# mLSTM's running maxima spread over the partitions by way of memory, attention masks joined to the maximum on VectorE

## The chip, the core and the metric

The kernel runs on one core of one Trainium2 chip. TensorE (PE) multiplies, VectorE (DVE), ScalarE (ACT) and GpSimd (POOL) compute elementwise and reduce, SyncE (SP) issues most of the loads. Each engine works through its own queue in order, and an instruction at the head of a queue that waits for another engine holds up everything behind it on that engine. The metric is the device time of one execution in microseconds (us).

## What is computed

One decoder layer on 256 positions of width 1024: three mixers side by side (a pooling mixer, an mLSTM with 4 heads, a block attention with 8 heads), an output product, and a feed-forward part with a short convolution. What the change touches are the mLSTM's decay weights and the attention's softmax. Cut to that:

```python
def step(carry, inp):                       # mLSTM, per head
    g = jnp.cumsum(lf, axis=-1)
    logd = jnp.where(causal, g[..., :, None] - g[..., None, :] + ic[..., None, :], -jnp.inf)
    inter = g + m[..., None]
    mt = jnp.maximum(inter, jnp.max(logd, axis=-1))
    w = jnp.einsum('bhtd,bhsd->bhts', qc, kc) * jnp.exp(logd - mt[..., None])
    ...
# attention, per head; at 256 positions there is one block, so the causal own block is all of it
    s_own = jnp.einsum('bhqd,bhkd->bhqk', qi, k_own) * scale
    s_own = jnp.where((kpos[None, :] <= qpos[:, None])[None, None], s_own, -jnp.inf)
    p = jax.nn.softmax(jnp.concatenate([s_sel, s_own], axis=-1), axis=-1)
```

With a(s) = i(s) - g(s) and M(t) the running maximum of a, a decay weight is exp(a(s) - M(t)) for s up to t, and 0 behind it.

## The kernel before

**Products.** Every float32 weight is split on ACT and DVE into a high part (`hi`, line 184) and a rest (`lo`, line 191), and each product is three matmuls: high by high, high by rest, rest by high. Weights come in units of about 1 MB by SP's queue into four buffers; a unit's load is issued when the rest of the unit four before it is made. The input product has eleven units ("of", "vi", "pool", "mq", "mk", "akA", "aqA", "akB", "aqB", "avA", "avB"); each is 4 blocks of 12 matmuls, called bulk blocks here. After them stand the output product (`wo`), the up product (`upr`, `up`) and the down product (`dn`).

**Order.** Between the bulk blocks the mixers' smaller work is woven in by hand. `put(key, f, *after)` registers a piece, the table `PLACE` gives it a number, and the pieces are emitted sorted by that number (a bulk block n has the number n). So one number sets where a piece's instructions come in the queue of every engine that it uses. The framework adds the semaphores and hands out buffers.

**mLSTM.** `gate_scans` (key "gs") makes, on 4 partitions, one per head, the running maximum `mr`. The decay weights need -M(t) on all 128 partitions (one partition per s, t along the row). For that `gate_hi` and `gate_lo` split `mr`, and for each head `decay_t` (keys ("pm", h)) runs four matmuls: a selector `sel_m` of -1 by the two parts, 384 columns each, and twice an identity by a bfloat16 mask of 128 columns. `decay` (("wt", h)) takes the exponential on ACT from PSUM into `wt`. `mscore_t` (("mS", j)) multiplies queries and keys of two heads, `mscore` (("me", h)) joins scores and decay on DVE, `mnum_t` (("mN", t)) multiplies by the values. `sigmoids` and `silu` make queries and keys ready; the sigmoids need a table load on ACT before and after.

**Pooling.** `pool_z` runs two chains of small adds on POOL, first j = 0, then j = 1; `pool_t` (("ply", j)) multiplies each result `pld` on PE, first j = 1, then j = 0.

**Attention.** `score_t` (("S", g, j)) makes scores of two heads: four float32 matmuls of 64 rows (two of 128 columns, two of 256) and four mask matmuls (identity by a bfloat16 mask, 128 columns). `prob_max` (("mx", g, j)) takes the row maxima on DVE straight from PSUM, `prob_exp` (("ex", g, j)) the exponentials on ACT from PSUM into `pr`, then come the division, the transposes (`PT`) and the product with the values (`O`). The masks and the selector come by one load into `con0` and are cast on POOL in `setup`.

Of the kernel before, what the change touches and what calls it, by code (L numbers as in the profile page):

```python
# [9 lines left out]
F32 = mybir.dt.float32  # L10
# [26 lines left out]
    "n1g": 3.714, "n1n": 4.567, "rbt": 6.601, "rb": 9.429, ("of", 0): 6.981, ("of", 1): 6.014, ("vi", 0): 6.19,  # L37
    ("vi", 1): 7.571, "setup": 3.741, "gain": 13.052, "pg": 7.69, "ga": 9.023, "gm": 9.583, "gs": 9.638, "gh": 9.938,
    "gl": 11.815, "gc": 11.24, "gco": 12.693, "gce": 15.533, ("ply", 0): 26.237, ("plh", 0): 26.457,
    ("pll", 0): 26.931, ("ply", 1): 22.154, ("plh", 1): 26.706, ("pll", 1): 27.325, ("plz", 0): 10.439,  # L40
# [10 lines left out]
    ("mlo", 1): 38.548, ("hq", "akA", 0): 21.853, ("hs", "akA", 0): 23.338, ("hq", "akA", 1): 23.685,  # L51
# [1202 lines left out]
```

## Time and profile before

| | |
|---|---|
| time, median of 3 runs | 314.48 us (314.48 to 314.83) |
| the profiled execution's own time | 314.26 us |
| its span, first to last instruction | 312.6 us |
| PE busy in the span | 308.1 us (99%) |
| DVE busy | 227.1 us (73%) |
| ACT busy | 186.0 us (59%) |
| POOL busy | 16.5 us (5%) |
| granted TensorE clock | 1.000 |

The profiled execution takes 1.66 us more than its span; that lies around it. Busy time is the time in which at least one instruction of the engine runs. Matmuls overlap: the 128x256 bulk matmul is listed with 0.28 us, but one starts every 0.12 us. So what a matmul costs on PE is read from the start of one row to the start of the next, not from its length. The mixers lie between 8 and 120 us, the up product up to 248 us, the down product behind it.

### The profile page before, as it was taken

Reading aid. Unit: us, or ns where it says so; the run is one execution under the profiler, and the core shown is the slowest. Engines: PE = TensorE matmul, PEld = TensorE weight load, DVE = VectorE, ACT = ScalarE, POOL = GpSimd, SP = SyncE. Lnnn points to the kernel's source line nnn. Section 1 sums busy time; section 2 is a strip of 40 time slices with the busy share of each in tenths; the row PEclk is TensorE's granted clock in tenths of the full one; section 3 lists DMA queues with packets and bytes.
Section 4 is the critical chain, followed back from the end, with each engine's and each line's share of the span. In section 5 each row is a group of like instructions: output and inputs, shape, how many; then the busy total and the mean of one; then the engine's idle time right before and its main releaser. Section 6 shows DMA issues by size and latency. Waiting matters only on the chain.

```text
span 312.6 us, 5639 instructions
## 1 busy us (share of the span) xinstructions
PE 308.1 (99%) x2251; PEld 283.7 (91%) x2251; DVE 227.1 (73%) x427; ACT 186.0 (59%) x366; POOL 16.5 (5%) x30
## 2 busy tenths in 40 slices
PE   8999999999999999999999999999999999999995
PEld 5999899989977789999999999999999988888885
DVE  1779898898746676689988888788788786534112
ACT  4986669688577536858566475565664594425000
POOL 0026910000000000000000000000000000000000
PEclk9999999999999999999999999999999999999999
DMA  7997553321703670161564464563555549800003
GB/s 227 424 411 282 191 214 136 134 66 72 268 2 136 240 297 2 39 232 53 217 229 177 148 236 156 173 235 134 204 200 151 228 151 368 316 0 2 0 0 134
DMA packets 8825, 53.81 MB, mean 172 GB/s; under 512 B 984, under 2 KB 1248, under 8 KB 2784
## 3 DMA queue, kind: packets, MB, share of 16 engines
q1 hardware_dynamic: 8512, 52.95, 45.6%
q10 hardware_dynamic: 288, 0.52, 0.6%
q8 instruction: 17, 0.28, 0.4%
q14 instruction: 8, 0.07, 0.1%
HBM read 52.42 MB, written 1.05 MB: 171 GB/s over the span
## 4 chain that ended last, share of the span: by engine, by line
PE 99%; DVE 0%; issue 0%
PE dn L842 20%; PE up L313 12%; PE up L311 12%; PE up L312 12%; PE wo L842 7%; PE warm L331 1%; PE upr L320 1%; PE upr L322 1%; PE upr L321 1%; PE of L455 1%; PE n1pt L350 1%; PE aqA L320 1%; PE mq L311 1%; PE mk L311 1%; PE akB L320 1%; PE vi L322 1%
## 5 line engine op out<-in xcount | busy, mean ns | idle before, releaser
L191 DVE TENSOR_TENSOR lo<-raw,hi 128x1024 fp32r<-128x1024 f32 (+2 forms) x102 | 116.1, 1158 | 24.7 <-ACT hi L184 24.6
L184 ACT ACTIVATE hi<-raw 128x1024 fp32r<-128x1024 f32 (+2 forms) x102 | 98.8, 994 | 28.5 <-PE dn L842 18.9
L311 PE MATMUL up<-h_hi,hi 128*128 128x256 f32 x320 | 90.4, 283 | 0.0
L313 PE MATMUL up<-h_hi,lo 128*128 128x256 f32 x320 | 90.3, 282 | 0.0
L312 PE MATMUL up<-h_lo,hi 128*128 128x256 f32 x320 | 90.1, 282 | 0.0
L311 PEld LDWEIGHTS up<-h_hi,hi 128*128 128x128 f32 x320 | 60.6, 189 | 0.0
L313 PEld LDWEIGHTS up<-h_hi,lo 128*128 128x128 f32 x320 | 60.5, 189 | 0.0
L312 PEld LDWEIGHTS up<-h_lo,hi 128*128 128x128 f32 x320 | 60.4, 189 | 0.0
L1103 DVE SCALAR_TENSOR_TENSOR fy<-up,par,fy 128x255 f32<-128x255 f32 x88 | 41.9, 481 | 14.9 <-ACT fy L1100 13.4
L1100 ACT ACTIVATE fy<-up,par 128x256 f32<-128x256 f32 x44 | 20.0, 465 | 31.9 <-PE up L313 31.9
L842 PE MATMUL dn<-hi,a_hi 128*128 128x512 f32 (+1 forms) x110 | 29.0, 349 | 0.0
L842 PE MATMUL dn<-hi,a_lo 128*128 128x512 f32 (+1 forms) x110 | 28.9, 348 | 0.0
L842 PE MATMUL dn<-lo,a_hi 128*128 128x512 f32 (+1 forms) x110 | 28.9, 348 | 0.0
L842 PEld LDWEIGHTS dn<-lo,a_hi 128*128 128x128 f32 x110 | 19.5, 188 | 2.9
L842 PEld LDWEIGHTS dn<-hi,a_lo 128*128 128x128 f32 x110 | 19.4, 188 | 2.9
L842 PEld LDWEIGHTS dn<-hi,a_hi 128*128 128x128 f32 x110 | 19.3, 188 | 2.9
L238 ACT ACTIVATE a_hi<-fy 128x256 fp32r<-128x256 f32 x22 | 9.2, 419 | 11.8 <-DVE fy L1109 11.8
L1152 DVE TENSOR_TENSOR xs<-dn,xs 128x512 f32<-128x512 f32 (+1 forms) x5 | 2.8, 583 | 16.5 <-PE dn L842 16.5
L842 PE MATMUL wo<-hi,mix_hi 128*128 128x512 f32 x32 | 11.4, 418 | 0.0
L842 PE MATMUL wo<-lo,mix_hi 128*128 128x512 f32 x32 | 10.7, 394 | 0.0
L842 PE MATMUL wo<-hi,mix_lo 128*128 128x512 f32 x32 | 10.6, 394 | 0.0
L239 DVE TENSOR_TENSOR a_lo<-fy,a_hi 128x256 fp32r<-128x256 f32 x22 | 9.2, 420 | 1.5 <-ACT a_hi L238 1.5
(307 smaller groups left out, 546.0 us busy)
## 6 DMA issues: line engine op xcount, KB each, us to landing
raw<-in_w SPq DMA_DIRECT2D x46, 1024.0 KB, 4.8
raw<-in_wg SPq DMA_DIRECT2D x2, 520.0 KB, 6.4
raw<-in_wg SPq DMA_DIRECT2D x1, 1040.0 KB, 8.8
out_y<-xs SPq DMA_DIRECT2D x3, 256.0 KB, 2.1
xs<-in_x ACTq DMA_DIRECT2D x2, 256.0 KB, 4.0
xs<-in_x SPq DMA_DIRECT2D x2, 256.0 KB, 4.0
con<-in_consts SPq DMA_DIRECT2D x1, 384.0 KB
par<-in_params SPq DMA_DIRECT2D x1, 337.0 KB, 10.6
```

The costliest lines, as they stand in the source:

```text
L184: nc.scalar.activation(hi_t[u][:, s], raw_t[u][:, s], AF.Copy)
L191: nc.vector.tensor_sub(lo_t[u][:, s], raw_t[u][:, s], hi_t[u][:, s].bitcast(F32))
L238: nc.scalar.activation(hi, src, AF.Copy)
L239: nc.vector.tensor_sub(lo, src, hi.bitcast(F32))
L311: nc.tensor.matmul(dst, a, h_hi[:, k, :], start=k == 0, stop=False)
L312: nc.tensor.matmul(dst, a, h_lo[:, k, :], start=False, stop=False)
L313: nc.tensor.matmul(dst, b, h_hi[:, k, :], start=False, stop=k == KT - 1)
L320: nc.tensor.matmul(dst, h_hi[:, k, ts_], hw[:, k, :], start=k == 0, stop=False)
L322: nc.tensor.matmul(dst, h_lo[:, k, ts_], hw[:, k, :], start=False, stop=k == KT - 1)
L842: nc.tensor.matmul(acc[t, c], a, b[:, k, o:o + n], start=st and i == 0, stop=sp and i == 2)
L1100: nc.scalar.activation(y, ps[j], AF.Copy, scale=pcol(c0 + 4 * NPAIR))
L1103: nc.vector.scalar_tensor_tensor(y[:, d:], ps[j][:, :S - d], pcol(c0 + 2 * NPAIR * tap), y[:, d:], op0=ALU.mult, op1=ALU.add)
```

## The change

The maxima no longer go through PE. `gate_scans` writes `mr` in another order, `spread_max` ("bm") stores it from POOL's queue to a buffer in memory, `spread_back` ("br") loads it from there, again from POOL's queue, as the same 1536 numbers into each of 128 partitions (786 KB, tile `mb`), and `mask_max` ("bs") sets the masked places with an AFFINE_SELECT on POOL, in place. `decay` takes the exponential in place of `mb`, with scale -1, and the scores are joined in `mb` too. `gate_hi`, `gate_lo` and `decay_t` go.

The attention's mask matmuls go as well. A mask of 256 columns is made once on POOL; `prob_max` becomes a TENSOR_TENSOR_REDUCE on DVE that adds the mask to the scores, writes the sum to `pr` in SBUF and takes the row maximum; `prob_exp` reads `pr` in place of PSUM. The load of `con0` goes, and the casts on POOL with it. Nearly all numbers of `PLACE` move a little.

```diff
-    ...("cy", "mk", 0): 19.109, ("ct", "mk", 0): 19.499, ("cz", "mk", 1): 19.365, ("cy", "mk", 1): 21.291,
...
+    "e": ..., ("hi", 1, 0): -2.6, "bm": 10.847, "br": 11.9, "bs": 13.467,
...
+    dpool = ctx.enter_context(tc.tile_pool(name="dpool", bufs=1, space=bass.MemoryType.DRAM))
...
-    nc.sync.dma_start(con0[:, :C_RCNT], consts[:, :C_RCNT])
-    nc.sync.dma_start(con, consts[:, C_RCNT:])
+    nc.sync.dma_start(con, consts)
...
+    mask = mpool.tile([P, S], F32, name="mask")
+    mb = mpool.tile([P, 3, 4, P], F32, name="mb")
...
-        nc.gpsimd.tensor_copy(mask_b, con0[:, C_MASK:C_MASK + 2 * P])
-        nc.gpsimd.tensor_copy(sel_m, con0[:4, C_SELM:C_SELM + 4 * P])
-        nc.gpsimd.tensor_copy(ident_b, ident)
+        nc.gpsimd.memset(mask, 0.0)
+        nc.gpsimd.affine_select(mask, mask, [[-1, S]], ALU.is_ge, NEG, base=P, channel_multiplier=1)
...
-    def gate_hi():
-        sb["mh"] = mpool.tile([4, 384], F32R, name="mh")
-        nc.scalar.activation(sb["mh"], sb["mr"], AF.Copy)
-
-    def gate_lo():
-        sb["ml"] = mpool.tile([4, 384], F32R, name="ml")
-        nc.vector.tensor_sub(sb["ml"], sb["mr"], sb["mh"].bitcast(F32))
+    def spread_max():
+
+        sb["far"] = dpool.tile([3, 4, P], F32, name="far")
+        nc.gpsimd.dma_start(sb["far"].rearrange("b h c -> h b c"), sb["mr"].rearrange("h (b c) -> h b c", c=P))
+
+    def spread_back():
+        nc.gpsimd.dma_start(mb, sb["far"].partition_broadcast(P))
+
+    def mask_max():
+
+        d = mb.rearrange("p b h c -> p (b h) c")[:, :8, :]
+        nc.gpsimd.affine_select(d, d, [[0, 8], [1, P]], ALU.is_ge, -NEG, base=0, channel_multiplier=-1)
...
-    def decay_t(h):
-
-        pm = aux([P, 384], f"pm{h}")
-        s = sel_m[:, h * P:(h + 1) * P]
-        nc.tensor.matmul(pm, s, sb["mh"], start=True, stop=False)
-        nc.tensor.matmul(pm, s, sb["ml"], start=False, stop=False)
-        for c in (0, S):
-            nc.tensor.matmul(pm[:, c:c + P], ident_b, mask_b[:, :P], start=False, stop=c == S)
-        ps_t["pm", h] = pm
-
     def decay(h):
-        pm = ps_t["pm", h]
-        e = mpool.tile([P, 384], F32, name=f"wt{h}")
-        nc.scalar.activation(e[:, :S], pm[:, :S], AF.Exp, bias=cols[:, 0, h:h + 1])
-        nc.scalar.activation(e[:, S:], pm[:, S:], AF.Exp, bias=cols[:, 1, h:h + 1])
+        e = mb[:, :, h, :]
+        nc.scalar.activation(e[:, 1:], e[:, 1:], AF.Exp, bias=cols[:, 0, h:h + 1], scale=-1.0)
+        nc.scalar.activation(e[:, 0], e[:, 0], AF.Exp, bias=cols[:, 1, h:h + 1], scale=-1.0)
         sb["wt", h] = e
...
     def score_t(g, j):
         q, k = sb["aq" + g, j], sb["ak" + g, j]
         pss = [aux([P, 384], f"S{g}{j}{half}") for half in range(2)]
-        for half in range(2):
-            hs = slice(64 * half, 64 * half + 64)
-            nc.tensor.matmul(pss[half][:, :P], q[hs, :P], k[hs, :P], start=True, stop=False)
-        for half in range(2):
-            nc.tensor.matmul(pss[half][:, :P], ident_b, mask_a, start=False, stop=True)
-        for half in range(2):
-            hs = slice(64 * half, 64 * half + 64)
-            nc.tensor.matmul(pss[half][:, P:], q[hs, P:], k[hs, :], start=True, stop=False)
-        for half in range(2):
-            nc.tensor.matmul(pss[half][:, S:], ident_b, mask_a, start=False, stop=True)
+        for o, t in ((slice(0, P), slice(0, P)), (slice(P, 384), slice(P, S))):
+            for half in range(2):
+                hs = slice(64 * half, 64 * half + 64)
+                nc.tensor.matmul(pss[half][:, o], q[hs, t], k[hs, :t.stop], start=True, stop=True)
...
     def prob_max(g, j):
...
+        pr = big(f"pr{g}{j}")[:, :768].rearrange("p (h c) -> p h c", c=384)
+        sb["pr", g, j] = pr
         for half in range(2):
             for t, s in spans:
-                nc.vector.tensor_reduce(mx[:, half, t:t + 1], pss[half][:, s], axis=AX.X, op=ALU.max)
+                nc.vector.tensor_tensor_reduce(pr[:, half, s], pss[half][:, s], mask[:, P - P * t:], 1.0, 3 * NEG,
+                                               op0=ALU.add, op1=ALU.max, accum_out=mx[:, half, t:t + 1])
...
     def prob_exp(g, j):
...
-                nc.scalar.activation(pr[:, half, s], pss[half][:, s], AF.Exp, bias=mx[:, half, t:t + 1],
+                nc.scalar.activation(pr[:, half, s], pr[:, half, s], AF.Exp, bias=mx[:, half, t:t + 1],
...
-    put("gh", gate_hi, "gs")
-    put("gl", gate_lo, "gh")
+    put("bm", spread_max, "gs")
+    put("br", spread_back, "bm")
+    put("bs", mask_max, "br")
...
-        put(("pm", h), do(decay_t, h), "gl", "setup")
-        put(("wt", h), do(decay, h), ("pm", h), "gco")
+        put(("wt", h), do(decay, h), "bs", "gco")
```

What the new numbers and pieces do to the engines' queues is seen at three places. In the rows below, an instruction stands with its line, its operation, what it writes and reads, and its shape; line numbers of the changed kernel are its own.

On PE, the first scores of the attention's second half (`SB`, two heads in two PSUM tiles), before:

```order
L322 MATMUL avA_1143<-hi_726,h_lo 128x256
L724 MATMUL SB_1197<-akBT_1166,aqBT_1163 128x128
L724 MATMUL SB_1198<-akBT_1166,aqBT_1163 128x128
L726 LDWEIGHTS ident_b
L726 MATMUL SB_1197<-mask_b,ident_b 128x128
L726 LDWEIGHTS ident_b
L726 MATMUL SB_1198<-mask_b,ident_b 128x128
L729 MATMUL SB_1197<-akBT_1166,aqBT_1163 128x256
L729 MATMUL SB_1198<-akBT_1166,aqBT_1163 128x256
```

and after:

```order
L318 MATMUL avB_1169<-hi_782,h_lo 128x256
L713 MATMUL SB_1184<-akBT_1136,aqBT_1085 128x128
L713 MATMUL SB_1185<-akBT_1136,aqBT_1085 128x128
L713 MATMUL SB_1184<-akBT_1136,aqBT_1085 128x256
L713 MATMUL SB_1185<-akBT_1136,aqBT_1085 128x256
L694 MATMUL hmT_1200<-ident,hm_835 128x128 x2
L316 MATMUL avB_1169<-hi_782,h_hi 128x256
```

The mask's four matmuls (two of them are behind the rows shown) are gone, the scores moved behind one more bulk block, and the mLSTM's transposes `hmT`, which stood by themselves before, now stand beside them. In the same way other woven-in pieces were put next to each other: outside the decay blocks, bulk work is broken into by 27 groups of small matmuls before and by 19 after.

On POOL, the end of pooling chain j = 0 (result `pld`) and the start of chain j = 1, before:

```order
L808 COPY plz_387<-plz_384 64x256
L811 TENSOR_TENSOR pld_391<-plz_387,con 128x256
L812 TENSOR_TENSOR pld_391<-pld_391,plz_381 128x256
L798 MEMSET plz_438 128x16
L804 MEMSET plz_441 128x16
L806 TENSOR_TENSOR plz_441<-plz_438 128x256
```

and after, where the second row of the round trip waits for the landing of the first:

```order
L792 COPY plz_372<-plz_369 64x256
L795 TENSOR_TENSOR pld_376<-plz_372,con 128x256
L796 TENSOR_TENSOR pld_376<-pld_376,plz_366 128x256
L605 DMA far<-mr 4x3x128
L608 DMA mb<-far 128x1536
L782 MEMSET plz_438 128x16
L788 MEMSET plz_441 128x16
L790 TENSOR_TENSOR plz_441<-plz_438 128x256
```

Both transfers now stand in the queue between the two chains; the AFFINE_SELECT on `mb` stands behind the second.

On ACT, the sigmoids (`sg`, between two table loads) and the decays, before:

```order
L642 ACTIVATE wt_645<-pm_562,cols 128x256
L643 ACTIVATE wt_645<-pm_562,cols 128x128
L524 ACTIVATE akAsq_651<-akA_616,n1r_236 128x256
L642 ACTIVATE wt_653<-pm_518,cols 128x256
L643 ACTIVATE wt_653<-pm_518,cols 128x128
L234 ACT_TABLE_LOAD
L494 ACTIVATE gm<-gm 128x256 x2
L497 ACTIVATE sg<-mqT_525 128x256
```

and after:

```order
L490 ACTIVATE sg<-mkT_617 128x256
L230 ACT_TABLE_LOAD
L630 ACTIVATE mb<-mb,cols 128x2x128
L631 ACTIVATE mb<-mb,cols 128x128
L630 ACTIVATE mb<-mb,cols 128x2x128
L631 ACTIVATE mb<-mb,cols 128x128
L517 ACTIVATE akAsq_653<-akA_587,n1r_253 128x256
```

All four heads' decays moved from ahead of the sigmoids to behind the second table load. On DVE each of the 16 maxima is two instructions now, the reduction and a read of its result (128x1).

## Rows read from the trace of the kernel before

**Rows 1.** The page, part 1: busy us (share) xinstructions of each engine.

```profile
PE 308.1 (99%) x2251; PEld 283.7 (91%) x2251; DVE 227.1 (73%) x427; ACT 186.0 (59%) x366; POOL 16.5 (5%) x30
```

**Rows 2.** Waits of PE: engine, line, waited for: us, times, longest.

```profile
PE warm L331 <- DVE idle L326: 1.3, 1, 1.3
```

**Rows 3.** Timeline of PE, first decay block: start us, length us, instruction, count.

```profile
30.39 0.28 PE L313 MATMUL mq<-h_hi,lo 128*128 128x256 f32 x1
30.60 0.44 PE L633 MATMUL pm<-mh,sel_m 4*128 4x384 f32 x1
...
31.24 0.36 PE L311 MATMUL mq<-h_hi,hi 128*128 128x256 f32 x1
31.44 0.28 PE L312 MATMUL mq<-h_lo,hi 128*128 128x256 f32 x1
31.55 0.28 PE L313 MATMUL mq<-h_hi,lo 128*128 128x256 f32 x1
```

**Rows 4.** Timeline of PE: one block of attention scores, and what follows.

```profile
82.28 0.49 PE L724 MATMUL SB<-akBT,aqBT 64*128 64x128 f32 x4
82.70 0.29 PE L726 MATMUL SB<-mask_b,ident_b 128*128 128x128 bf16 x2
82.92 0.70 PE L729 MATMUL SB<-akBT,aqBT 64*128 64x256 f32 x4
83.56 0.29 PE L731 MATMUL SB<-mask_b,ident_b 128*128 128x128 bf16 x2
83.65 0.36 PE L320 MATMUL avB<-hi,h_hi 128*128 128x256 f32 x1
```

**Rows 5.** Timeline of PE: the pooling product, and both blocks of mLSTM scores.

```profile
46.61 0.59 PE L817 MATMUL ply<-pld,par 128*128 128x256 f32 x2
...
49.98 0.93 PE L653 MATMUL mS<-mqT,mkT 64*128 64x256 f32 x8
50.84 0.39 PE L320 MATMUL aqA<-hi,h_hi 128*128 128x256 f32 x1
...
52.45 1.10 PE L653 MATMUL mS<-mqT,mkT 64*128 64x256 f32 x8
```

**Rows 6.** Timeline of POOL: ends of chain j = 0 and of chain j = 1.

```profile
30.57 1.62 POOL L812 TENSOR_TENSOR pld<-pld,plz 128x256 f32<-128x256 f32 x1
...
39.27 0.81 POOL L812 TENSOR_TENSOR pld<-pld,plz 128x256 f32<-128x256 f32 x1
```

**Rows 7.** DMA issues: tile, queue, count, KB each, median us to landing.

```profile
xs<-in_x ACTq DMA_DIRECT2D x2, 256.0 KB, 4.0
...
con<-in_consts SPq DMA_DIRECT2D x1, 256.0 KB, 12.7
out_y<-xs SPq DMA_DIRECT2D x2, 128.0 KB, 1.7
```

**Rows 8.** Timeline of DVE around the mLSTM's scores, with the idle time before a row.

```profile
28.44 0.96 DVE L614 TENSOR_TENSOR ml<-mr,mh 4x384 fp32r<-4x384 f32 x1
...
48.89 0.43 DVE L501 TENSOR_TENSOR mqT<-mqT,sg 128x256 f32<-128x256 f32 x1 [0.63 <-ACT sg L497]
...
51.70 0.42 DVE L530 TENSOR_REDUCE akAss<-akAsq 128x4 f32<-128x256 f32 x1
52.03 0.55 DVE L658 SCALAR_TENSOR_TENSOR wt<-mS,wt 128x384 f32<-128x384 f32 x1
52.49 0.17 DVE L535 TENSOR_SCALAR akAss<-akAss 128x8 f32<-128x8 f32 x1
```

**Rows 9.** Groups by line and shape: xcount, busy us, mean ns, idle us before.

```profile
L739 DVE TENSOR_REDUCE mxA<-SA 128x1 f32<-128x256 f32 x4 | 1.7, 414 | 0.0
...
L751 ACT ACTIVATION_READ_ACCUMULATOR prA<-SA,mxA,aqr 128x1 f32 x8 | 1.7, 210 | 0.0
...
L210 POOL TENSOR_SCALAR_AFFINE_SELECT ident<-ones 128x128 f32<-128x128 f32 x1 | 0.3, 292 | 0.1
```

**Rows 10.** One stretch: busy us of PE, PEld, DVE, ACT, POOL; clock; DMA share, GB/s.

```profile
28.00:75.00 47.00, 47.00 (x382) 43.50 (x381) 42.00 (x104) 35.93 (x80) 11.50 (x16) 1.00 0.43 157
```

More of the change, by code (lines that the diff above doesn't have):

```diff
@@ L36 @@
 PLACE = {
[L37 to L40, printed above, removed]
[10 rows of a table removed]
-    ("mlo", 1): 38.548, ("hq", "akA", 0): 21.853, ("hs", "akA", 0): 23.338, ("hq", "akA", 1): 23.685,
[44 rows of a table removed]
+    "n1g": 4.19, "n1n": 4.722, "rbt": 7.381, "rb": 8.32, ("of", 0): 6.657, ("of", 1): 5.837, ("vi", 0): 6.566,
+    ("vi", 1): 7.27, "setup": 3.875, "gain": 16.963, "pg": 7.867, "ga": 8.38, "gm": 9.124, "gs": 9.606, "gc": 10.156,
+    "gco": 12.183, "gce": 16.746, ("ply", 0): 26.237, ("plh", 0): 27.301, ("pll", 0): 27.489, ("ply", 1): 22.756,
+    ("plh", 1): 26.859, ("pll", 1): 27.39, ("plz", 0): 9.748, ("plz", 1): 12.359, ("cz", "mq", 0): 14.116,
[54 rows of a table added]
 }
@@ L108 @@
 N_UNITS = U_DOWN + N_DOWN
-C_MASK = 0
-C_SELM = C_MASK + 2 * P
-C_RCNT = C_SELM + 4 * P
+C_RCNT = 0
 C_END = C_RCNT + 2 * S
@@ L206 @@
     par = cpool.tile([P, Q_END], F32, name="par")
-    con0 = tpool.tile([P, D], F32, tag="big", name="con0", bufs=3)
-    con = mpool.tile([P, C_END - C_RCNT], F32, name="con")
+    con = mpool.tile([P, C_END], F32, name="con")
     nc.gpsimd.memset(ones, 1.0)
@@ L411 @@
     mix_lo = mpool.tile([P, KT, S], F32R, name="mix_lo")
-    mask_b = mpool.tile([P, 2 * P], BF16, name="mask_b")
-    mask_a = mask_b[:, P:]
-    sel_m = mpool.tile([4, 4 * P], F32R, name="sel_m")
-    ident_b = mpool.tile([P, P], BF16, name="ident_b")
+    mask = mpool.tile([P, S], F32, name="mask")
+    mb = mpool.tile([P, 3, 4, P], F32, name="mb")
     gg = mpool.tile([P, 1], F32, name="gg")
@@ L602, in gate_scans @@
         nc.vector.scalar_tensor_tensor(ar, ps_t["pg"][:, 0, :], b_i, gc, op0=ALU.add, op1=ALU.subtract)
-        nc.vector.tensor_tensor_scan(mr[:, :S], ar, ar, 0.0, op0=ALU.max, op1=ALU.max)
-        nc.vector.tensor_copy(mr[:, S:], mr[:, P:S])
-        nc.vector.tensor_add(gc, gc, mr[:, :S])
+        nc.vector.tensor_tensor_scan(mr[:, P:], ar, ar, 0.0, op0=ALU.max, op1=ALU.max)
+        nc.vector.tensor_copy(mr[:, :P], mr[:, S:])
+        nc.vector.tensor_add(gc, gc, mr[:, P:])
         sb["mr"] = mr
-    def gate_hi():
-        sb["mh"] = mpool.tile([4, 384], F32R, name="mh")
-        nc.scalar.activation(sb["mh"], sb["mr"], AF.Copy)
-    def gate_lo():
-        sb["ml"] = mpool.tile([4, 384], F32R, name="ml")
-        nc.vector.tensor_sub(sb["ml"], sb["mr"], sb["mh"].bitcast(F32))
+    def spread_max():
[6 more added lines that the diff above has]
+        nc.gpsimd.affine_select(d, d, [[0, 8], [1, P]], ALU.is_ge, -NEG, base=0, channel_multiplier=-1)
     def gate_cols_t():
@@ L647, in mscore_t @@
         for half in range(2):
-            ps_t["mS", 2 * j + half] = aux([P, 384], f"mS{2 * j + half}")
+            ps_t["mS", 2 * j + half] = aux([P, 3, P], f"mS{2 * j + half}")
         q, k = sb["mq", j], sb["mk", j]
-        for s, o in ((0, slice(0, S)), (1, slice(S, 384))):
+        for s, o in ((0, slice(1, 3)), (1, 0)):
             for half in range(2):
@@ L664, in mnum_t @@
             if t == 0:
-                nc.tensor.matmul(pn[:, h, :], e[:, :P], v_aug[:, 0, h, :], start=True, stop=True)
+                nc.tensor.matmul(pn[:, h, :], e[:, 1], v_aug[:, 0, h, :], start=True, stop=True)
             else:
-                nc.tensor.matmul(pn[:, h, :], e[:, P:S], v_aug[:, 0, h, :], start=True, stop=False)
-                nc.tensor.matmul(pn[:, h, :], e[:, S:], v_aug[:, 1, h, :], start=False, stop=True)
+                nc.tensor.matmul(pn[:, h, :], e[:, 2], v_aug[:, 0, h, :], start=True, stop=False)
+                nc.tensor.matmul(pn[:, h, :], e[:, 0], v_aug[:, 1, h, :], start=False, stop=True)
         ps_t["num", t] = pn
@@ L745, in prob_exp @@
     def prob_exp(g, j):
-        pss, rq, mx = ps_t["S", g, j], sb["rq", g], sb["mx", g, j]
+        pr, rq, mx = sb["pr", g, j], sb["rq", g], sb["mx", g, j]
         sm = tpool.tile([P, 2, NT], F32, tag="sm", name=f"sm{g}{j}")
-        pr = big(f"pr{g}{j}")[:, :768].rearrange("p (h c) -> p h c", c=384)
         for half in range(2):
             for t, s in spans:
-                nc.scalar.activation(pr[:, half, s], pss[half][:, s], AF.Exp, bias=mx[:, half, t:t + 1],
+                nc.scalar.activation(pr[:, half, s], pr[:, half, s], AF.Exp, bias=mx[:, half, t:t + 1],
                                      scale=rq[:, t, 2 * j + half:2 * j + half + 1],
@@ L1223, in _consts @@
     c = np.zeros((P, C_END), np.float32)
-    i = np.arange(P)
-    c[:, C_MASK:C_MASK + P] = np.where(i[None, :] >= i[:, None], 0.0, NEG)
-    c[:, C_MASK + P:C_MASK + 2 * P] = np.where(i[None, :] <= i[:, None], 0.0, NEG)
-    for h in range(4):
-        c[h, C_SELM + P * h:C_SELM + P * (h + 1)] = -1.0
     t = np.arange(S) + 1.0
```

108 rows, old and new, of the table PLACE are left out of this document.

## The prediction, made blind

> **What bounds the kernel now.** I read the busy times first: PE is busy 308.1 of 312.6 us [rows 1]. Then the waits: PE waited once, 1.3 us at the very start [rows 2]. Between 28 and 75 us, where all of the mLSTM and half of the attention lie, it is busy in all 47.00 us, and the granted clock is 1.00 [rows 10]. So PE sets the time, by its amount of work: what is taken from PE comes off the time, whatever moves to other engines is free as long as PE still finds its inputs, and each microsecond in which it doesn't is lost. The second thing to see is how near the next engine is: DVE is busy 42.0 of those 47 us [rows 10]. Third, the places where PE arrives just in time, since the change makes it arrive earlier.
>
> **What leaves PE.** *Decay blocks.* From the first selector matmul to the next bulk matmul 31.24 - 30.60 = 0.64 us pass [rows 3]. Bulk matmuls start every 0.11 us (31.44 to 31.55), but the block's first one starts 0.21 after the one ahead, and the second bulk matmul behind it 0.20 after the first: going from one kind of matmul to another costs 0.10 and 0.09 us more. A block is 0.83 us, and there are four: 3.3 us. If the switches stayed, 4 x 0.64 = 2.6.
>
> *Mask matmuls.* A score block takes 83.65 - 82.28 = 1.37 us [rows 4]. The mLSTM's scores are the same four matmuls (64 rows, twice 256 and twice 128 columns) without masks: 50.84 - 49.98 = 0.86 us [rows 5]. So 0.51 goes with the masks, 4 x 0.51 = 2.0 us. Least: the mask rows by themselves, (82.92 - 82.70) + (83.65 - 83.56) = 0.31 [rows 4], in all 1.2. Most: group A's two blocks stand side by side, so one pair of switches (0.19) can fall out besides, 2.2.
>
> *Pieces put side by side.* Bulk work is broken into 19 times, not 27. A break costs up to the 0.19 of two switches, 8 x 0.19 = 1.5; nothing where the neighbours differ in kind (transposes beside 64-row or 64-column matmuls), as in about half of these. I take 0.6, from 0 to 1.5.
>
> Together 3.3 + 2.0 + 0.6 = 5.9 us less work on PE (3.8 to 7.0).
>
> **What moves to GpSimd, and who waits.** The round trip stands in POOL's queue between the two pooling chains. The first transfer waits for `mr`, which is long there. The second waits for the landing of the first, and behind it in the queue stand chain j = 1 and then the AFFINE_SELECT. That chain's result is wanted first on PE, at 46.61 [rows 5]; now it is ready at 39.27 + 0.81 = 40.08 [rows 6], 6.5 us ahead. After the change PE comes there earlier by the decay blocks, all four of which lie ahead, and one merged break: 46.61 - 3.3 - 0.2 = 43.1. POOL comes later by the round trip: one issue, one landing, one more issue. No POOL transfer is in this trace. The nearest landing is a small write to memory by another queue, 1.7 us for 128 KB; a load of 256 KB took 4.0 [rows 7]. An issue costs POOL between nothing and its slowest add here, 1.62 [rows 6]. That is 1.7 to 7.2 us; as the transfer is 6 KB I stay near the short end, 3.5. Chain j = 0 ends at 30.57 + 1.62 = 32.2, chain j = 1 takes 40.08 - 32.2 = 7.9, so it ends at 32.2 + 3.5 + 7.9 = 43.6, and PE waits 0.5 (0 to 4.2).
>
> The page "DMA: Bandwidth & Descriptors" of the Trainium skill, section "Anatomy of one DMA — SWDGE (gpsimd) path", gives a transfer issued by GpSimd a fixed cost of about 2.0 us and attributes most of it to the write's receipt; no run here shows it yet. By it the chain would end near 43 and this wait would be nil.
>
> The AFFINE_SELECT takes 0.29 us for 128 columns [rows 9], so at most 8 x 0.29 = 2.3 for 1024, and the decays can start on ACT at about 46. They stand behind the sigmoids' second table load, so ACT is hardly sooner there. The load into `mb` has those 7.9 us of chain j = 1 to land; a quarter less than a weight unit, it is covered.
>
> **What moves on DVE.** `ml` goes, 0.96 us [rows 8]. Each of 16 maxima gets a read of its result. The nearest row for that is ACT's, 0.21; the reduction itself reads PSUM as before (0.41 for 256 columns) and now writes a row and reads a mask as well [rows 9]. I take 0.2 each, 3.2 us, half of it (1.6) in the crowded stretch; from 1.6 to 4.8 in all. Covered, in the second half, by the slack of a DVE that isn't full there; in the first by little.
>
> The place where it shows first is the second block of mLSTM scores. One of its PSUM tiles comes free when the first `mscore` is done; before, that ended at 52.49 [rows 8] with PE there at 52.45 [rows 5]: already just in time, its block 1.10 long where the first was 0.93. PE now comes 3.5 earlier, 48.95. On DVE, up to that point, `ml` goes (0.96), one head reduction moves behind it (51.70 to 52.03, 0.33), and part of the 0.63 that DVE waited for sigmoids [rows 8] and of its other idle time, 5.0 us in the stretch [rows 10]; the count of splits ahead of it (ten from 25 us on) is the same. So `mscore` ends 1.3 to 3.5 us earlier, say 2.3: at 50.2, and PE waits 1.2. This wait comes after the one for POOL and holds what is left of it, so the larger counts, not the sum: 1.2 us, from 0 to 4.2. ACT's exponentials read SBUF in place of PSUM, same size, no change taken. The load taken out (384 KB) and the one put in (786 KB) run beside loads that use 0.43 of the engines' time [rows 10]: 0.
>
> **The sum.** 5.9 - 1.2 = 4.7 us. On the profiled execution, 314.26 - 4.7 = 309.6 (span 312.6 - 4.7 = 307.9); the median of the runs lies 0.2 above it, so 314.48 - 4.7 = **309.8 us**. About 0.2% (0.6 us) is what a measurement of this kernel can tell from no change.
>
> **Rivals.** *All waits stay covered* (POOL's issues near nothing, DVE gains all of its idle time): 314.48 - 5.9 = 308.6, with the bounds of the work 307.5 to 308.6. For it: 6.5 us of margin now. Against: the 52.45 block is late already. Chance 0.15 for under 308.6.
>
> *The round trip becomes PE's wait.* A round trip of 6 us ends the chain at 46.1 and costs PE 3.0: 311.6; one of 7.2, the upper bound, 4.2: 312.8. For it: a landing and two issues that no row prices. Against: 6 KB, written while DMA is half free. Chance 0.15 for 311.4 to 313.8.
>
> *Slower: the landing is as long as at the start of the program*, where a 256 KB load took 12.7 us [rows 7]. POOL blocks for 12.7 + 1.6, chain j = 1 ends at 54.4, PE waits 11.3: 314.48 - 5.9 + 11.3 = 319.9. It decides from a round trip of 43.1 - 32.2 - 7.9 + 5.9 = 8.9 us on. Against: that load queued behind megabytes of others, while around 32 us the engines are half free [rows 10]. Chance 0.05.
>
> *No change: DVE becomes the bound.* It would, if the 5.0 us that it idles between 28 and 75 us are all chains that don't shrink. Then the stretch takes 47.0 - 1.0 + 1.6 = 47.6 and PE's savings in it are lost; behind it remain two score blocks and some merged breaks, about 1.3: 314.48 + 0.6 - 1.3 = 313.8, and with the maxima at their upper price (2.4) 314.6. For it: 42 of 47. Against: at least 0.63 of the idle time is a wait that the new order removes, and splits can slip to a later place, since they stand some microseconds ahead of their use. Chance 0.05.
>
> **How the numbers follow.** The forecast's own range, with waits up to 3 and the work's bounds, is 308.6 to 311.4, chance 0.60. With the covered case (0.15), the late round trip (0.15), the DVE case (0.05) and the slower one (0.05) all is counted. 8 in 10 need 308.0 to 312.6: that leaves out the far ends of the first two rivals, and both last. Faster by over 0.2% (under 313.85): 0.60 + 0.15 + 0.15 and a part of the DVE case, 0.91. Within 0.2%: 0.04. Slower: 0.05.
>
> **What would show it.** Between `mq` and `akA` PE has no breaks, so that `akA` starts near 38.9, not 42.3. A score block with no masks lasts 0.9, not 1.37. On POOL the gap between the end of chain j = 0 and the first add of chain j = 1 is the round trip: 3.5 expected. PE's waits then list `ply` on POOL with under 1 us and the second `mS` on DVE with 1 to 2; nothing else above 0.5. DVE's maxima with their reads cost 0.2 each more than before. The prediction is wrong if that gap is over 6, if PE waits at the attention's transposes or scores, or if the score blocks keep their 1.37 (then the masks' switches were not theirs).

## The result, and the profile after

| | before | after |
|---|---|---|
| median of the runs, us | 314.48 | 313.09 |
| profiled execution, span | 312.6 | 311.4 |
| PE busy in the span | 308.1 | 304.1 |

The ratio is 0.9946, 95% interval 0.9931 to 0.9962: 1.4 us faster (lowest run 312.29, highest 313.34). 309.8 was forecast, with a range up to 312.6; the direction was right, the size was not, and the time lies half a microsecond outside. One execution of `e9_mask_early` below, at a granted clock of 0.56 throughout and 494 us, is in no median.

First the busy times (columns as in [rows 1]) and the waits (as in [rows 2]) of the changed kernel:

```profile
PE 304.1 (98%) x2219; PEld 282.6 (91%) x2219; DVE 228.0 (73%) x442; ACT 186.4 (60%) x365; POOL 17.6 (6%) x32
```

```profile
POOL mb L608 <- DMA far<-mr: 5.3, 1, 5.3
...
PE ply L801 <- POOL pld L796: 2.7, 1, 2.7
```

PE has one new wait, the pooling product on POOL; beside the wait at the very start [rows 2], DVE appears nowhere in its list. POOL itself waits 5.3 us for the landing of `far`. Its timeline shows the round trip, between the end of chain j = 0, the two transfers, and chain j = 1 (compare [rows 6]):

```profile
32.48 1.61 POOL L796 TENSOR_TENSOR pld<-pld,plz 128x256 f32<-128x256 f32 x1
34.03 0.78 POOL L605 DMA_DIRECT2D far<-mr  x1
40.11 0.58 POOL L608 DMA_DIRECT2D mb<-far  x1 [5.30 <-DMA far<-mr]
...
40.89 0.61 POOL L790 TENSOR_TENSOR plz<-plz 128x256 f32<-128x256 f32 x1
...
45.35 0.78 POOL L796 TENSOR_TENSOR pld<-pld,plz 128x256 f32<-128x256 f32 x1
46.25 1.92 POOL L613 TENSOR_SCALAR_AFFINE_SELECT mb<-mb 128x1024 f32<-128x1024 f32 x1
```

From 34.09 to 40.68 is 6.6 us of round trip; chain j = 1 ends at 46.13. On PE's timeline the rows that answer to [rows 4] and [rows 5] are:

```profile
39.09 0.28 PE L316 MATMUL akA<-hi,h_hi 128*128 128x256 f32 x1
...
43.25 0.28 PE L318 MATMUL akA<-hi,h_lo 128*128 128x256 f32 x1
46.19 0.70 PE L801 MATMUL ply<-pld,par 128*128 128x256 f32 x2 [2.65 <-POOL pld L796]
...
48.10 0.41 PE L318 MATMUL akA<-hi,h_lo 128*128 128x256 f32 x1
48.31 0.41 PE L316 MATMUL akA<-hi,h_hi 128*128 128x256 f32 x1
...
83.50 0.93 PE L713 MATMUL SB<-akBT,aqBT 64*128 64x128 f32 x8
84.36 0.44 PE L694 MATMUL hmT<-ident,hm 128*128 128x128 f32 x2
```

`akA` begins at 39.09, where 38.9 was forecast; a score block lasts 84.36 - 83.50 = 0.86 us. So PE's work went as forecast. Then comes the wait, and a second loss: at 48 us bulk matmuls start every 0.21 us, not every 0.12. Two stretches of after (columns as in [rows 10]), and then one of the kernel before:

```profile
34.00:40.00 6.00, 6.00 (x53) 6.00 (x52) 5.75 (x11) 2.94 (x5) 0.81 (x2) 1.00 0.95 327
47.20:50.40 3.20, 3.20 (x17) 3.20 (x16) 3.20 (x5) 2.37 (x8) 0.97 (x1) 0.50 0.03 5
```

```profile
34.00:40.00 6.00, 6.00 (x47) 5.22 (x46) 5.02 (x8) 4.92 (x10) 5.69 (x8) 1.00 0.92 314
```

Behind the wait the granted clock is 0.50 (1.2 GHz) for about 3.4 us: 3.4 x (1 - 0.12 / 0.21) = 1.5 us lost. And the DMA engines are busy 0.95 of the stretch in which `far` is to land; they were busy 0.92 of it before the change too. At the place where the prediction put the transfer, 32.2 us, they were all but idle in the kernel before:

```profile
32.20:34.00 1.80, 1.80 (x14) 1.41 (x14) 1.80 (x3) 0.01 (x1) 1.73 (x5) 1.00 0.02 5
```

Between 31 and 34 us one weight load was issued before, at 33.4; in the changed kernel two are, at 31.8 and 33.5, and `far` comes at 34.03, behind both.

How much work left PE follows from a stretch that holds all of the change, from the first `mq` matmul to the transposes behind the mixer; first and last row of it, before and after:

```profile
27.54 0.39 PE L311 MATMUL mq<-h_hi,hi 128*128 128x256 f32 x1
...
132.75 0.49 PE L1056 MATMUL up<-ident,upc 128*128 128x128 f32 x3
```

```profile
27.68 0.28 PE L307 MATMUL mq<-h_hi,hi 128*128 128x256 f32 x1
...
131.35 1.18 PE L1040 MATMUL up<-ident,upc 128*128 128x128 f32 x8
```

It is 105.21 us long before and 103.67 after: 1.54 less, with 2.65 of wait and some 1.5 of half clock in it. That makes 5.7 us less work; 5.9 was forecast. The half clock in this sum is an estimate; the same stretch in three runs below in which the clock held gives 5.2 (`e1_swap_ply`), 5.3 (`e7_probes`) and 5.9 (`e2_fill`, without its fill).

### The profile page after: what moved, and what is told of

Same layout as the page of the kernel before. It is cut to its first block, busy times and chain, and to the rows that moved or that the text cites. A ratio compares the mean times of both kernels' runs of the same rounds, so it can differ in the third digit from the quotient of the medians.

```text
span 311.4 us, 5585 instructions
## 1 busy us (share of the span) xinstructions
PE 304.1 (98%) x2219; PEld 282.6 (91%) x2219; DVE 228.0 (73%) x442; ACT 186.4 (60%) x365; POOL 17.6 (6%) x32
## 4 chain that ended last, share of the span: by engine, by line
PE 90%; POOL 4%; DMA 2%; DVE 1%; ACT 1%; issue 1%; POOLq 0%
PE dn L826 20%; PE up L309 12%; PE up L307 12%; PE up L308 12%; PE wo L826 7%; POOL plz L790 2%; DMA far<-mr 2%; PE warm L327 1%; PE upr L316 1%; PE upr L318 1%; PE upr L317 1%; PE of L448 1%; PE n1pt L346 1%; PE aqA L316 1%; POOL pld L795 1%; POOL pld L796 1%
```

## Experiments

The theory from this profile: the work is gone, and 4.2 us of the gain are lost at one place, the wait for POOL and the fall of the clock behind it. The rivals: DVE would have taken the place of that wait; the clock fell for another reason; the landing is that long by itself. Medians are of five to twelve runs unless said; those of the kernel before beside them are 314.55 to 314.61.

### The attention's part alone, and the decays' part alone

`e4_attn_only` is the kernel before with these lines, and `prob_exp` reading `pr`:

```diff
-            nc.tensor.matmul(pss[half][:, :P], ident_b, mask_a, start=False, stop=True)
-            nc.tensor.matmul(pss[half][:, S:], ident_b, mask_a, start=False, stop=True)
-                nc.vector.tensor_reduce(mx[:, half, t:t + 1], pss[half][:, s], axis=AX.X, op=ALU.max)
+                nc.vector.tensor_tensor_reduce(pr[:, half, s], pss[half][:, s], mask[:, P - P * t:], 1.0, 3 * NEG,
+                                               op0=ALU.add, op1=ALU.max, accum_out=mx[:, half, t:t + 1])
```

> The kernel before, with only the attention masks changed as in the change: no mask matmuls in the score blocks, the mask added in the maximum's instruction on DVE, the exponential read from that row. Decays and order as before. Theory: each of four score blocks falls from 1.37 to 0.86 us, DVE's 16 maxima cost at most 0.2 each more and stay covered: 314.5 - 2.0 = 312.5 us. Rival: DVE, full in this stretch, holds PE by what it takes on (up to 3.2 us): 313.5 to 315, with a PE wait on DVE at the attention's transposes or scores.

312.84 us, ratio 0.9946 (0.9934 to 0.9958): 1.7 less. PE waits for nothing but at the start.

`e6_masks_too` is the changed kernel with the mask matmuls back on PE:

```diff
+            nc.tensor.matmul(pss[half][:, :P], ident_b, mask_a, start=False, stop=True)
+            nc.tensor.matmul(pss[half][:, S:], ident_b, mask_a, start=False, stop=True)
```

> The changed kernel, with the attention's mask matmuls put back on PE as in the kernel before, besides the masks on DVE, which stay (a place masked twice is as far below the maximum). This is the change without what it takes from PE in the attention. Theory: the two parts add up; four score blocks cost 0.51 more each, as the kernel before with only the attention changed gained 1.7: 313.1 + 1.7 to 2.0 = 314.8 to 315.1 us, so the decay part alone, with the waits it brings, gains nothing. Rival: PE's added work sits beside waits and part of it is covered: 313.5 to 314.5.

315.10 us, ratio 1.0026 (1.0003 to 1.0049), with a wait of 3.9 us for POOL. The two parts add up within the noise: the attention's part is worth 1.7; the rest, for all that it takes from PE (3.5 us in the profiled execution, by the stretch above), gains nothing and costs 0.5 (0.1 to 1.5). Its runs fall in two groups by the mean granted clock: six of 0.998 and over took 313.9 to 314.6, six of 0.995 and under 315.6 to 317.2. So whether the clock falls differs from run to run of one kernel, and even where it held the rest of the change gained at most 0.7.

### The clock and the wait

`e2_fill` gives PE something to do ahead of the late product:

```diff
         py = aux([P, S], f"ply{j}")
+        for _ in range(20 if j else 0):
+            nc.tensor.matmul(py, idle[:, :P], idle[:, :S], start=True, stop=True)
```

> The changed kernel, with twenty matmuls of 256 columns on zeros (about 2.1 us of PE) issued ahead of the pooling product of chain j = 1, into the tile that the product then overwrites. The wait for POOL is as long, but PE works through most of it. Theory: the fall of the granted clock to 0.5 from 47.1 to 50.5 us comes from PE's idle 2.7 us. Then the listed wait falls to about 0.5, the clock stays 1.00, the loss of 1.6 us goes and the wait itself stays: 311.5 us. Rival: the clock falls for another reason at this place, and the fill changes nothing: 313.1 us, with a stretch at 0.5 again. If the fill runs past the end of the chain, the time is longer by that.

311.99 us, 1.1 under the changed kernel by the medians, 0.7 by the ratios (0.9924, 0.9909 to 0.9940), whose intervals just overlap. In the profiled execution the chain ended 1.4 us later than in after's, and PE still waited 1.8 us, now behind the fill, so that this execution took 313.03, as long as after's; the same stretch as above is at full clock (PE's timeline, then the window):

```profile
43.49 2.36 PE L802 MATMUL ply<-idle 128*128 128x256 bf16 x20
47.62 0.70 PE L803 MATMUL ply<-pld,par 128*128 128x256 f32 x2 [1.77 <-POOL pld L796]
```

```profile
47.20:50.40 3.20, 2.78 (x21) 2.73 (x22) 3.20 (x4) 2.01 (x6) 1.60 (x2) 1.00 0.03 5
```

All six executions have a mean clock of 0.999 or more, where the five of the changed kernel have 0.995 or less. So with 20 useless matmuls in the wait the clock holds: it fell because PE stood still. That cost about 1 us, by the rows 1.5.

### What the landing is made of

`e7_probes` (one run) adds five round trips in the layout of `far`, but read back into four partitions, at the end of POOL's queue, where nothing waits for them:

```diff
+        for i in range(5):
+            nc.gpsimd.dma_start(t.rearrange("b h c -> h b c"), src.rearrange("h (b c) -> h b c", c=P))
+            nc.gpsimd.dma_start(nxt.rearrange("h (b c) -> h b c", c=P), t.rearrange("b h c -> h b c"))
```

> The changed kernel, with five more round trips at the end of GpSimd's queue, from about 48 us on, where nothing waits for GpSimd: a write of 6 KB in the layout of `far`, then a read of it back into four partitions, each after the landing of the one before. Their waits price a landing where the DMA engines do little (no load between 43 and 50 us) and where loads run. Theory: the 5.3 us belong to packets that stand behind weight loads (the DMA engines are busy 0.95 of 34 to 40 us); in the quiet stretch a landing takes 2 to 3 us from the end of the issue, beside loads 4 to 6. Rival: the landing is that long by itself: over 4.5 us everywhere. The time is near 313.1, as PE waits for none of it.

POOL's timeline: each row's last bracket is the wait for the landing of the transfer one row above.

```profile
50.11 0.59 POOL L623 DMA_DIRECT2D pb<-pf  x1 [1.49 <-DMA pf<-rows]
56.20 0.59 POOL L620 DMA_DIRECT2D pf<-pb  x1 [5.49 <-DMA pb<-pf]
58.33 0.59 POOL L623 DMA_DIRECT2D pb<-pf  x1 [1.54 <-DMA pf<-pb]
...
66.16 0.59 POOL L620 DMA_DIRECT2D pf<-pb  x1 [3.00 <-DMA pb<-pf]
```

Windows over these four waits (the last two columns are the DMA share and GB/s):

```profile
48.60:50.10 1.50, 1.50 (x15) 1.20 (x14) 1.50 (x3) 1.50 (x5) 0.02 (x1) 1.00 0.10 15
50.70:56.20 5.50, 5.17 (x40) 4.68 (x40) 5.18 (x18) 4.50 (x10) 0.01 (x2) 1.00 0.55 192
...
63.10:66.20 3.10, 3.10 (x29) 3.10 (x28) 2.83 (x21) 2.01 (x8) 0.10 (x2) 1.00 0.62 258
```

```profile
56.80:58.30 1.50, 1.50 (x16) 1.50 (x15) 1.50 (x5) 1.44 (x3) 0.00 (x0) 1.00 0.02 4
```

The same 6 KB take 1.5 us where the DMA engines are idle and 3.0 and 5.5 where a weight load is in flight; of the nine waits the other five are 1.5 to 1.6, one of them (61 to 62.5 us) at a share of 0.39. Both long ones are for the read back (`pb`); no probe's write met a full load, but `far`, a write of the same layout, did in every run at its old place, and in `e8_far_first` below it meets none. Taken together, the landing is short by itself and long only beside a load. The run took 311.86 us: PE's wait for the chain was 2.0 us in it, `far` itself cost 4.7, and the clock did not fall.

`e3_sp_queue` sends the round trip by another queue:

```diff
-        nc.gpsimd.dma_start(sb["far"]...
+        nc.sync.dma_start(sb["far"]...
-        nc.gpsimd.dma_start(mb, ...
+        nc.sync.dma_start(mb, ...
```

> The changed kernel, with both transfers of the round trip issued by SP in place of GpSimd, at the same place in the order. GpSimd then waits for no landing: chain j = 1 follows chain j = 0 at 34.1 and takes 5.4 to 7.9 us, so it ends at 39.5 to 42, ahead of PE's 43.4. Theory: no PE wait over 0.5 us, clock 1.00, 308.8 us. The landing of `far` seen from SP tells whether the 5.3 us belong to GpSimd's queue (then it is near the 1.7 to 2.2 us of other small transfers) or to the transfer (then near 5). Rival: SP is held by its wait for that landing, the weight loads behind it come later, and PE waits for a split: over 310 us, with a wait on DVE or ACT at a bulk product.

313.54 us, no better than the change. SP issued `far` at 27.7 and `mb` at 32.2, so the landing took about 4.2 by this queue as well. But there `far` stood right behind a weight load of the same queue, issued at 27.3 and landed at about 32.0, so this run doesn't separate the queue from the load. Chain j = 1 was done at 41.5, and the wait for POOL was gone. But PE waited 2.2 us for DVE's `silu` at the first block of mLSTM scores and twice 0.7 at the second, and the clock fell behind that. Neither theory nor rival had these places.

### What waits behind the wait

`e1_swap_ply` exchanges the two pooling products on PE:

```diff
-    ("ply", 0): 26.237, ("ply", 1): 22.756
+    ("ply", 0): 22.756, ("ply", 1): 26.237
```

> The changed kernel, with only PE's two pooling products exchanged: PE asks for chain j = 0 at the early place (ready at 34.1 us) and for chain j = 1 some 10 us later, where it is long done. POOL, DVE and ACT keep their orders. Theory: what the prediction missed is one place, PE's wait of 2.7 us for chain j = 1 and the 1.6 us that the half clock behind that wait costs. Then no PE wait over 0.5 us is left, the granted clock stays 1.00 between 28 and 75 us, and the time is 313.1 - 4.3 = 308.8 us. Rival: the next late thing takes the place of the wait, the mask on POOL (48.2) with the decays behind it on ACT and the first `mscore` on DVE, for which the second block of mLSTM scores waits; PE would come there near 49.3, `mscore` could end near 50 to 51: 309.5 to 311 us, with that wait in the list.

311.94 us, ratio 0.9918 (0.9907 to 0.9930), 1.2 under the changed kernel by the medians, 0.9 by the ratios. The theory failed. The rival was right that another late thing takes the place of the wait, but hardly as to which, and the time is 0.9 above its range. PE's waits:

```profile
PE mS L641 <- DVE mqT L494: 1.7, 1, 1.7
...
PE mS L641 <- ACT mb L630: 0.7, 1, 0.7
...
PE mS L641 <- DVE mb L646: 0.3, 1, 0.3
```

The 1.7 at the first block are for `silu`. The 0.7 at the second are put down to ACT's decays, but the score matmuls don't read those. They read the last `silu`, whose end, 51.48, lies 0.15 us ahead of PE's start (DVE's row, then PE's):

```profile
51.07 0.41 DVE L494 TENSOR_TENSOR mkT<-mkT,sg 128x256 f32<-128x256 f32 x1
```

```profile
51.63 0.67 PE L641 MATMUL mS<-mqT,mkT 64*128 64x256 f32 x2 [0.74 <-ACT mb L630]
```

In `e5_pool_late` the lag is the same 0.15, and the list there names `silu`. So only the 0.3, for the first `mscore`, belong to the rival's path of mask and decays.

`e5_pool_late` puts the mask ahead of chain j = 1 on POOL and gives that chain until 58 us (the chain is a piece of its own, with own tiles):

```diff
+        put(("plc", j), do(pool_c, j), ("plz", j), at=(9.75, 13.6)[j])
-    ("ply", 1): 22.756
+    ("ply", 1): 27.6
```

> The changed kernel, with GpSimd's order changed: the AFFINE_SELECT stands ahead of pooling chain j = 1, and PE's two pooling products are exchanged and the later one put some 3 us later still (near 58 us), so that the chain has until then. The chain's tiles get buffers of their own, so that no other engine waits for them. With the products only exchanged, PE waited 1.7 us for DVE's `silu` and 0.9 at the second block of mLSTM scores, because DVE's convolution taps took 0.75 each while GpSimd ran chain j = 1, 0.49 while it did not. Theory: DVE and GpSimd slow each other; with GpSimd waiting for the landing during the taps, the last six take 2.9 in place of 4.5 us, `silu` comes 1.5 to 2.4 us earlier, PE's waits at the scores fall under 1 us in all: 309.3 to 310.2 us. Rival: the taps' length has another cause, they keep 0.75 and PE keeps its 2.7 us: 312 us.

314.00 us (0.9969 to 1.0013): no faster than before. Yet the mechanism is there. DVE's timeline, the six convolution taps of `mk`, first in `e1_swap_ply`, where POOL runs chain j = 1 beside them, then here, where POOL waits for a landing:

```profile
41.91 4.50 DVE L478 SCALAR_TENSOR_TENSOR mkT<-mkz,par,mkT 128x255 f32<-128x255 f32 x6
```

```profile
41.24 2.94 DVE L478 SCALAR_TENSOR_TENSOR mkT<-mkz,par,mkT 128x255 f32<-128x255 f32 x6
```

A tap takes 0.75 us beside POOL's adds, 0.49 alone. The first block of scores then waited for nothing. But the mask came only at 48.1, since `mb` landed 6.8 us after its issue, and chain j = 1 now ran beside `silu` and the splits: PE waited 1.3 (for `silu`) and 0.9 (for the first `mscore`) at the second block, and the clock fell.

`e8_far_first` issues `far` ahead of chain j = 0, and nothing else:

```diff
-    "bm": 10.847
+    "bm": 9.65
```

> The changed kernel, with the first transfer of the round trip put ahead of pooling chain j = 0 in GpSimd's queue; its source is ready near 25 us, where no load is under way. PE's products are not exchanged. Theory: the landing is covered by chain j = 0, GpSimd issues the second transfer without a wait, chain j = 1 ends at 41 to 42.5, ahead of PE's 43.4, no wait at the pooling product, no clock fall there; what is left are DVE's waits at the scores as with the products exchanged (2 to 3 us, as GpSimd and DVE now meet in other places): 311.3 to 312.3 us. Rival: the landing takes longer than chain j = 0 (over 8 us) or chain j = 1 is as slow as before the change (7.9): a wait for POOL stays and the time is near 313.

313.61 us, above both bounds. `far` is the same write as in the change, now issued where no load is in flight; its issue here and in the change (columns as in [rows 7]), and the window of its landing here:

```profile
far<-mr POOLq DMA_DIRECT2D x1, 6.0 KB, 1.9
```

```profile
far<-mr POOLq DMA_DIRECT2D x1, 6.0 KB, 5.8
```

```profile
25.50:27.50 2.00, 2.00 (x19) 1.85 (x18) 2.00 (x4) 0.93 (x1) 1.96 (x4) 1.00 0.05 15
```

1.9 us against 5.8, at a DMA share of 0.05 against 0.95. DVE is busy for all of this window, so a busy DVE alone doesn't hold the landing up. The landing was covered, POOL never waited for it, chain j = 1 ended at 41.0 and PE did not wait for it. PE waited 2.1 us for `silu` on DVE, whose taps now ran beside POOL for all of chain j = 1, and the clock fell from 49.5 to 52.9. The estimate left that fall out.

`e9_mask_early` joins both (first transfer, chain j = 0, second transfer, mask, chain j = 1) and puts PE's product near 66 us; `e10_chain_late` also holds chain j = 1 back:

```diff
+            nc.gpsimd.tensor_copy(gate, sb["mk", 1][:, :1])
```

> The changed kernel, with GpSimd's order first transfer, chain j = 0, second transfer, AFFINE_SELECT, chain j = 1, and with PE's product of chain j = 0 at the early place and that of chain j = 1 near 66 us. So no landing is waited for that isn't covered, the mask is ready near 42.5 us, well ahead of ACT, and PE waits for no chain. Chain j = 1 runs from about 42.5 to 48 us, beside DVE's last taps and its `silu`. Theory: what is left is DVE and GpSimd slowing each other in that stretch: taps 0.75 in place of 0.49, PE's waits at the two blocks of mLSTM scores 1 to 2 us in all: 310.0 to 311.5 us. Rival: with mask and landing out of the way nothing waits: 308.6 to 309.5.

> As e9_mask_early, and chain j = 1 is held back until DVE has multiplied the last of the mLSTM's `mk` by its sigmoid (a copy of one column of that result stands ahead of the chain on GpSimd), so it runs after about 49 us and not beside the taps. Theory: the work taken from PE was 5.9 us all along, and the waits that ate it were the landing behind weight loads, the mutual slowing of DVE and GpSimd and the clock that fell after a wait. With these out of the way PE's waits at the scores are under 0.7 us in all and the time is 314.5 - 5.9 + 0.3 to 0.7 = 308.9 to 309.4 us. Rival: DVE is the bound of this stretch by its own work: waits at the scores of 2 us or more stay, 310.5 to 312.

`e9_mask_early` took 313.17 us, above theory and rival; its one trace is of the 494 us execution, so where it lost is open. `e10_chain_late` took 311.84, ratio 0.9908 (0.9895 to 0.9920), the lowest median here, about level with `e1_swap_ply`. Its PE waits:

```profile
PE mS L641 <- ACT mb L630: 0.6, 1, 0.6
PE akB L316 <- ACT aqAsq L517: 0.6, 1, 0.6
```

Besides these, 0.3 at the second block for DVE and 0.3 at the attention's transposes. The 0.6 at the scores are again the last `silu`'s (it ends at 50.02, PE starts at 50.17). The wait at the scores is 0.9, not under 0.7, and new small ones stand behind it, for squares, head sums and quotients that come from ACT and DVE. So with the three causes out of the way PE waits for POOL no more and the clock holds, but the theory's 308.9 to 309.4 are missed by 2.4 us or more. The listed waits are 1.7 of that; the rest, about 1 us, no row here explains. The time lies in the rival's range, without the rival's waits of 2 us.

`e11_silu_first` and `e12_splits_behind` move two weight splits on DVE, behind `silu` and behind the first `mscore`:

```diff
-    ("lo", 7, 1): 22.606, ("lo", 8, 0): 23.292
+    ("lo", 7, 1): 24.35, ("lo", 8, 0): 24.4      (e11_silu_first)
+    ("lo", 7, 1): 24.96, ("lo", 8, 0): 24.97     (e12_splits_behind; last silu at 23.4)
```

> As e10_chain_late, with two weight splits on DVE moved behind the last two `silu` multiplications (2.35 us of splits, used by PE some 10 us later). Theory: the second block of mLSTM scores then waits for the decays and the first `mscore` alone; 0.3 us less waiting than e10_chain_late or the same: 308.6 to 309.4 us. Rival: the splits, and the weight load that starts behind them, come too late, and PE waits at a bulk product: 310 us or more.

> As e10_chain_late, with DVE's order changed as e11_silu_first meant to and didn't: there the two weight splits (2.35 us) went behind the `silu` multiplications but stood ahead of the first `mscore`, which then began at 51.4 us and cost PE 2.0 us at the second block of mLSTM scores. Here they stand behind that `mscore` too. Theory: what PE waits for at this block is set by what stands ahead of the first `mscore` in DVE's queue; it then ends near 49.5 us and that wait falls under 0.4 us (0.9 in e10_chain_late). The splits now delay the head sums of group A, so the waits of 0.6 and 0.3 us at a bulk product and at the attention's transposes stay or grow by some tenths: 310.8 to 311.6 us. Rival: the splits only move the delay, and PE loses as much at the later places: 311.8 or more.

313.00 and 315.34 us: both worse than `e10_chain_late`. In the first, the wait for the last `silu` was gone, but PE waited 2.0 us for the first `mscore`, behind which the splits should have stood. In the second the rival held; PE's longest waits behind the start are

```profile
PE akB L316 <- DVE knA L549: 2.7, 1, 2.7
...
PE mS L641 <- DVE mb L646: 0.9, 1, 0.9
```

and the clock fell behind the 2.7. The delay went to the next user of DVE.

## Why the prediction was wrong, step by step

- **What leaves PE: right.** `akA` at 39.09 (38.9 forecast), score blocks of 0.86 (0.9), in all 5.7 us by the sum above, 5.2 to 5.9 by the other runs (5.9). The attention's part alone gave 1.7, between the 1.2 and the 2.0 of that step.
- **The round trip: mis-sized, and that is the step that failed.** The bounds, 1.7 to 7.2 us, held 6.6; I took 3.5, "as the transfer is 6 KB". Size wasn't what decides. The wait for the landing is 1.5 us with idle DMA engines and 4.0 to 5.7 in every run in which POOL writes `far` at this place, with a load in flight. So 3.5 was near the price of a quiet trip (0.8 of issue, 1.5 of wait, 0.6 of issue: 2.9). The DMA share that I leaned on, 0.43 [rows 10], is a mean over 47 us, and so is the "half free" in the case against the slower rivals. At 32.2 the engines were idle in the kernel before (0.02), from 34 on they were full (0.92): the transfer came 1.9 us later than I had it and met the loads. The gap is over the 6 us that the prediction named as its sign of being wrong. PE's wait for POOL was 2.65, where 0.5 was forecast and DVE's 1.2 went into the sum.
- **The second rival described the result, in part by luck.** "A round trip of 6 us ends the chain at 46.1 and costs PE 3.0: 311.6": it ended at 46.13, cost 2.65, and with the clock's 1.5 us the rival's sum is 313.1. But its 46.1 is 32.2 + 6 + 7.9, and measured were 34.09, 6.6 and 5.4. A load 2 us behind the transfer's place was reason to give it more than 0.15.
- **The clock was put at nothing, and it weighs as much as the wait.** Of the 3.3 us between 309.8 and 313.1, 2.65 - 1.2 = 1.45 are the wait and 1.5 the clock behind it. [rows 10] show 1.00, and I read it as given. In the change it fell behind the wait; with the wait filled, in `e2_fill`, it stayed at 1.00.
- **Two errors on POOL that nearly cancel.** Chain j = 0 ended 1.9 us later than 32.2 and chain j = 1 took 5.4 in place of 7.9. Its 128x256 adds took 1.5 us before, beside DVE's splits, and 0.6 to 0.7 after, beside the convolution taps, so a chain's length can't be moved to another time unchanged.
- **DVE's wait: the wrong piece, hidden in the result.** 1.2 us were forecast at the second block for the first `mscore`; with POOL's wait out of the way (`e1_swap_ply`) that was 0.3. `silu` was missed at both blocks: 1.7 at the first, though [rows 8] show one still running at 48.89 and PE was to arrive near 46.5, and 0.7 at the second. So even with a short round trip the time would probably have been near the 311.9 of `e1_swap_ply`, not 309.8.
- **DVE's maxima: cheaper than bounded.** The page's groups of after (columns as in [rows 9]):

```profile
L723 DVE CUSTOM_DVE_ANT_0 prA<-SA,mask 128x256 f32<-128x256 f32 x4 | 1.7, 420 | 0.0
...
L723 DVE DVE_READ_ACCUMULATOR2_ANT mxA<- 128x1 f32 x8 | 0.7, 84 | 0.0
```

  Mask and written row are free (0.42 against 0.41 us), the read is 0.084, not 0.2: 16 x 0.084 = 1.3 us in all, where 1.6 was the lower bound.
- **Covered, but only just:** the load of `mb` landed 6.1 us after its issue, when chain j = 1 had just ended; in `e7_probes` the mask waited 0.8 for it.

On the fixed cost of about 2.0 us that the Trainium skill gives for a GpSimd transfer (page "DMA: Bandwidth & Descriptors", section "Anatomy of one DMA — SWDGE (gpsimd) path"): the quiet probes agree, 0.59 of issue and 1.5 of wait; at the place of the change it was 0.78 and 5.3, so the measurement decides.

## What to carry to other kernels

Price a transfer by the DMA share of the very microseconds in which it must land and of the few behind them, not by its size or by the stage's mean: a small shift can put it into the next load. A round trip between two pieces of an in-order queue costs everything behind it, so look for the next asker first. When PE sets the time, a wait can cost more than its length: here the clock fell behind it. Exchanging two products, or 20 useless matmuls, each got back about 1 us. And before counting a saving, walk PE's new arrival times past every producer: here three (POOL, `silu`, the first `mscore`) were late for them, by 2.7 us in the change, 1.7 and 0.3 in `e1_swap_ply`.

## What the runs showed of the hardware

- The granted clock fell to 0.50, in the change for about 3.4 us, behind PE's waits of 2.7 us (after, `e12_splits_behind`), 3.9 (`e6_masks_too`), 2.1 (`e8_far_first`), 2.2 with twice 0.7 (`e3_sp_queue`) and 1.3 with 0.9 (`e5_pool_late`), and not behind 2.0 (`e7_probes`, `e11_silu_first`), 1.7 with 0.7 and 0.3 (`e1_swap_ply`) or 1.8 that followed a fill (`e2_fill`). Runs of one kernel differ: `e12_splits_behind` took 313.8 to 314.2 us at a mean clock of 0.999 and over, 315.1 to 315.6 at 0.995 and under.
- DVE and POOL slow each other, and which loses more depends on the pair. A tap on DVE with two SBUF inputs took 0.75 us beside POOL's adds and 0.49 without; the adds took 0.61 to 0.67 beside it. Beside DVE's splits an add of 128x256 took 1.49 before the change, a split 1.43, where one took 1.22 with POOL waiting. The Trainium skill (page "SBUF — State Buffer", section "Who interferes with whom") says that a DVE instruction with two SBUF inputs contends with a GpSimd instruction that reads SBUF; the trace agrees.
- A write of 6 KB to memory from POOL's queue landed 1.9 us after its issue with idle DMA engines and 5.8 beside 1 MB loads.
